# Linear attention on one core: K and V of the last two groups in one load each, Q group by group

## The chip, the core and the metric

The kernel runs on one core of a Trainium2 chip. A core has a matrix engine (TensorE, PE in the profile), three engines for elementwise work (VectorE or DVE, ScalarE or ACT, GpSimd or POOL), and SyncE (SP), which here only issues transfers. Sixteen DMA engines move data between device memory (HBM) and the on-chip memory (SBUF). The engines run side by side and wait for each other through semaphores. The metric is the device time of one execution in microseconds (us); lower is better.

## The reference

Attention without a softmax: Q and K pass through a feature map, and the sums over the sequence are taken first.

```python
# Q, K, V: (8, 12, 512, 64) float32
Q_feat = np.maximum(0, Q) + 1
K_feat = np.maximum(0, K) + 1
KV = np.einsum('bhkd,bhkv->bhdv', K_feat, V)
K_sum = np.sum(K_feat, axis=2)
numerator = np.einsum('bhqd,bhdv->bhqv', Q_feat, KV)
denominator = np.einsum('bhqd,bhd->bhq', Q_feat, K_sum)
return (numerator / (denominator[:, :, :, None] + 1e-10)).astype(np.float32)
```

For each of the 96 heads, K and V give one 64x64 matrix and one vector of 64; Q is multiplied by both, and the first result is divided by the second.

## The kernel before

The 96 heads are worked off in 12 groups of eight heads (`NG` = 12). One group of Q, K or V is 1 MB of float32 in HBM; the load converts it to bf16, so 512 KB arrive in SBUF. One group of the output is 1 MB of float32.

**Loads.** `load` (lines 93 to 103) starts one transfer per tensor from the POOL queue, in the order K, V, Q, for one group or for two at once. The destination is half of a tile, or a whole one, of a pool with two buffers for each tensor (`IN_BUFS` = 2); a tile holds two groups, so a pair of groups reuses the buffer of the pair before the last. `load_pair(s)` (line 105) loads groups 2s and 2s + 1: for the pairs 1 to 4 with one transfer for each tensor (2 MB read), for the last pair, groups 10 and 11, group by group: K10, V10, Q10, K11, V11, Q11, each 1 MB read. (Group 0's K is loaded as float32 from SP by `load_first_k`; V and Q of group 0 and all of group 1 are transfers of their own at the start.) A transfer on the POOL queue has one of eight semaphores, which are used in turn, so a transfer may be issued only when the eighth one before it has landed.

**Work of a group g.** `k_features` and `q_features` (two DVE instructions each, line 122), `v_blocks` (V copied into a block layout, three copies on DVE, line 140, and one on ACT, line 138), `keys_values` (32 matmuls into PSUM, line 157, then ACT moves the sums into `kva_diag`), `transposes` (16 on PE, line 176, each half copied by ACT, line 177), `output` (four times: matmuls into PSUM, line 189, then on DVE a reciprocal, line 199, and a multiplication into `o_sb`, line 200). There are two PSUM buffers for the four parts of `output`, so parts three and four need DVE to be done with parts one and two.

**Order.** The program order is written out by hand under `tc.manual_schedule()`, and each engine follows it strictly. In step g of the main loop the calls are: K features, V blocks and Q features of g, transposes of g - 1, output of g - 2, keys-and-values of g, then (after odd g) the load of the pair that takes the freed buffers, then the store of g - 3. So the loads of groups 10 and 11 stand after the work of step 7. The last group is written out after the loop, with its Q features moved behind the output of group 9.

**Stores.** `store(g)` sends groups 0 to 9 from the POOL queue as one transfer each, and groups 10 and 11 from SP in two halves each. `o_sb` has six buffers (`OUT_BUFS`).

The pair tile is split by `own(g)`; the users of a group wait for the transfer that brought it:

```python
            nc.gpsimd.dma_start(
                out=t[:, ms], in_=drams[x][:, 2 * groups[0] : 2 * groups[-1] + 2]
            )
            for g in groups:
                raw[x, g] = t[:, own(g)]
```

Of the kernel before, what the change touches and what calls it, by code (L numbers as in the profile page):

```python
# [19 lines left out]
def kernel(  # L20
# [64 lines left out]
    def own(g):  # L85
        return slice(g % 2 * 2, g % 2 * 2 + 2)
# [6 lines left out]
    def load(s, groups, names="kvq"):  # L93
        ms = slice(groups[0] % 2 * 2, groups[-1] % 2 * 2 + 2)
        for x in names:
            if (x, "buf", s) not in raw:
                raw[x, "buf", s] = in_pool.tile([P, 4, C2, D], BF16, name=f"{x}_raw")
            t = raw[x, "buf", s]
# [6 lines that stand above are left out]
    def load_pair(s):  # L105
        if s < NG // 2 - 1:
            load(s, (2 * s, 2 * s + 1))
        else:
            load(s, (2 * s,))
            load(s, (2 * s + 1,))  # L110

    def store(g):
        o_sb = outs.pop(g)
# [104 lines left out]
    with tc.manual_schedule():  # L218
# [11 lines left out]
        for t in kva_diag:  # L230
            nc.gpsimd.memset(t, 0.0)
        load_pair(1)
        clear(5, 7, 9)
        for g in range(NG - 1):
            k_features(g)
            v_blocks(g)
            q_features(g)
            if g:
                transposes(g - 1)
            if g >= 2:  # L240
                output(g - 2)
            keys_values(g)
            if g % 2 and g // 2 + 2 < NG // 2:
                load_pair(g // 2 + 2)
            if g >= LAG:
                store(g - LAG)
# [42 lines left out]
```

## Time and profile before

| | before |
|---|---|
| median of 7 runs | 127.21 us (126.61 to 127.89) |
| the profiled execution | 127.06 us |
| its span | 125.3 us |
| granted TensorE clock, mean | 0.823 |
| DVE busy | 88.4 us (71%) |
| ACT busy | 68.0 us (54%) |
| PE busy | 68.2 us (54%) |
| POOL busy | 27.4 us (22%) |
| HBM read, written | 37.75 MB, 12.58 MB (402 GB/s over the span) |

The span is from the first to the last instruction that the profile shows; the execution's own time is 1.8 us longer. A line of the timeline reads: start and duration in us, engine, line of the kernel, operation, destination <- source, shapes, and how many instructions are merged; in brackets, how long the engine had been idle and what ended the wait. For a transfer the duration is that of the issuing instruction, not of the data; when the data landed is asked for separately, by tile. The rows of digits are the share of busy time in 40 equal slices of the span, in tenths; GB/s counts the bytes as written.

### The profile page before, as it was taken

The page shows a single profiled execution, that of the slowest core. Times are in us where ns is not written, and L with a number is a line of the kernel's source. Part 1 is how long each engine was busy: PE and PEld are TensorE (multiplying, and loading weights), DVE is VectorE, ACT ScalarE, POOL GpSimd, SP SyncE. Part 2 cuts the span into 40 slices and gives each one's busy share as a digit, 9 for nine tenths or more (in the row PEclk, how much of TensorE's full clock was granted, in tenths as well). Part 3 has the DMA queues.
Part 4 walks back from the last instruction along what each step waited for, and adds up shares of the span by engine and source line. Part 5 has one row for each costly group of instructions (what it writes and reads, how often), then busy time and mean ns, then how long its engine had stood idle before and what let it go on. Part 6 is the DMA issues. An engine that isn't in the chain of part 4 may idle for free.

```text
span 125.3 us, 2337 instructions
## 1 busy us (share of the span) xinstructions
PE 68.2 (54%) x960; PEld 50.7 (40%) x960; DVE 88.4 (71%) x188; ACT 68.0 (54%) x87; POOL 27.4 (22%) x43
## 2 busy tenths in 40 slices
PE   0005959000049694797847969104978569694500
PEld 0004648000036573556635748003656447482200
DVE  4896280206099998995999985619979999758920
ACT  7832198006700889609796197670079871987000
POOL 6990213000002091020900224203321102020000
PEclk9999999965556999558997799955599967999955
DMA  3999999999999999999999999999999999999993
GB/s 73 343 214 209 211 209 212 213 208 210 210 216 212 211 210 215 212 211 210 242 408 311 209 209 213 211 345 394 228 211 211 213 263 414 421 418 411 402 399 118
DMA packets 13419, 32.13 MB, mean 256 GB/s; under 512 B 608, under 2 KB 608, under 8 KB 13408
## 3 DMA queue, kind: packets, MB, share of 16 engines
q0 software_dynamic: 12048, 28.84, 98.6%
q1 hardware_dynamic: 1360, 3.15, 6.8%
q8 instruction: 7, 0.11, 0.3%
q14 instruction: 4, 0.03, 0.1%
HBM read 37.75 MB, written 12.58 MB: 402 GB/s over the span
## 4 chain that ended last, share of the span: by engine, by line
DMA 69%; DVE 13%; issue 6%; POOL 3%; PE 3%; POOLq 0%; DVEq 0%
DMA out_dram<-o_sb 36%; DMA q_raw<-in_Q_dram 24%; DMA v_raw<-in_V_dram 10%; DVE o_sb L200 8%; DVE v_all L140 2%; POOL v_raw L99 2%; PE kva_ps L157 2%; DVE recip L199 1%; PE qt_ps L176 1%; POOL q_raw L99 1%; PE o_ps L189 1%; POOL out_dram L116 1%; DVE qf L122 1%; DVE kf L122 1%; POOL k_raw L99 0%
## 5 line engine op out<-in xcount | busy, mean ns | idle before, releaser
L157 PE MATMUL kva_ps<-v_all,kf 128*64 128x320 bf16 x384 | 38.4, 370 | 12.2 <-DVE v_all L140 10.7
L189 PE MATMUL o_ps<-kva_diag,qt 128*64 128x130 bf16 x384 | 19.7, 239 | 38.2 <-DVE o_sb L200 37.7
L157 PEld LDWEIGHTS <-kf 128*64 128x64 bf16 x384 | 26.9, 139 | 20.4 <-DVE v_all L140 12.1
L200 DVE TENSOR_TENSOR o_sb<-o_ps,recip 128x512 f32<-128x512 f32 x48 | 33.2, 692 | 1.6
L140 DVE COPY v_all<-v_raw 32x2048 bf16<-32x2048 bf16 x36 | 26.5, 737 | 10.1 <-DMA v_raw<-in_V_dram 9.7
L189 PEld LDWEIGHTS <-qt 128*64 128x64 bf16 x384 | 13.0, 117 | 43.8 <-DVE o_sb L200 42.0
L177 ACT COPY qt<-qt_ps 128x1024 bf16<-128x1024 bf16 x24 | 29.7, 1309 | 0.3
L138 ACT COPY v_all<-v_raw 32x2048 bf16<-32x2048 bf16 x12 | 22.7, 1894 | 11.8 <-DMA v_raw<-in_V_dram 11.6
L167 ACT CAST kva_diag<-kva_ps 64x256 bf16<-64x256 f32 x24 | 8.9, 372 | 34.2 <-PE kva_ps L157 34.1
L122 DVE TENSOR_SCALAR qf<-q_raw 128x1024 bf16<-128x1024 bf16 x24 | 9.1, 423 | 6.5 <-DMA q_raw<-in_Q_dram 6.3
L99 POOL DMA_DIRECT2D k_raw<-in_K_dram x7 | 5.3, 764 | 37.8 <-DVE kf L122 37.8
L176 PE MATMUL qt_ps<-identity,qf 128*128 128x128 bf16 x192 | 13.5, 226 | 0.0
L199 DVE RECIPROCAL recip<-o_ps 128x8 f32<-128x8 f32 x48 | 9.6, 199 | 5.3 <-PE o_ps L189 5.3
L122 DVE TENSOR_SCALAR kf<-k_raw 128x1024 bf16<-128x1024 bf16 x22 | 8.7, 438 | 6.0 <-DMA k_raw<-in_K_dram 6.0
L116 POOL DMA_DIRECT2D out_dram<-o_sb x10 | 8.1, 810 | 21.9 <-DVE o_sb L200 16.3
L176 PEld LDWEIGHTS <-qf 128*128 128x128 bf16 x192 | 11.5, 102 | 3.5 <-issue 3.2
L99 POOL DMA_DIRECT2D v_raw<-in_V_dram x8 | 6.0, 754 | 19.7 <-ACT v_all L138 16.3
L99 POOL DMA_DIRECT2D q_raw<-in_Q_dram x8 | 5.9, 743 | 4.2 <-DMA q_raw<-in_Q_dram 4.2
L213 DVE MEMSET v_all<- 128x3072 f32 (+1 forms) x2 | 4.4, 2192 | 1.1 <-DVE ones L225 0.7
L168 ACT CAST kva_diag<-kva_ps 64x4 bf16<-64x4 f32 x24 | 4.0, 168 | 0.0
L214 ACT COPY v_all<-zero 128x2048 f32<-128x2048 f32 x2 | 3.7, 1894 | 0.0
L214 ACT ACT_TABLE_LOAD x1 | 1.3, 1283 | 0.7 <-PEq L273 0.7
(12 smaller groups left out, 4.6 us busy)
## 6 DMA issues: line engine op xcount, KB each, us to landing
out_dram<-o_sb POOLq DMA_DIRECT2D x10, 1024.0 KB, 19.5
k_raw<-in_K_dram POOLq DMA_DIRECT2D x4, 1024.0 KB, 18.2
v_raw<-in_V_dram POOLq DMA_DIRECT2D x4, 1024.0 KB, 20.6
q_raw<-in_Q_dram POOLq DMA_DIRECT2D x4, 1024.0 KB, 24.7
v_raw<-in_V_dram POOLq DMA_DIRECT2D x4, 512.0 KB, 15.9
q_raw<-in_Q_dram POOLq DMA_DIRECT2D x4, 512.0 KB, 16.7
out_dram<-o_sb SPq DMA_DIRECT2D x4, 512.0 KB, 5.1
k_raw<-in_K_dram POOLq DMA_DIRECT2D x3, 512.0 KB, 22.1
```

Source lines behind the costliest of these rows:

```text
L99: nc.gpsimd.dma_start(out=t[:, ms], in_=drams[x][:, 2 * groups[0] : 2 * groups[-1] + 2])
L116: nc.gpsimd.dma_start(out=o_to, in_=o_sb)
L122: nc.vector.tensor_scalar(out=dst, in0=src, scalar1=1.0, scalar2=1.0, op0=ALU.add, op1=ALU.max)
L138: nc.scalar.copy(out=v_blk[g % 2][ps, b], in_=v_raw[ps])
L140: nc.vector.tensor_copy(out=v_blk[g % 2][ps, b], in_=v_raw[ps])
L157: nc.tensor.matmul(kva_ps[64 * n : 64 * n + 64], lhsT=kf[:, c, n, :], rhs=vb[:, :, n, c, :], start=(c == 0), stop=(c == C2 - 1),)
L167: nc.scalar.copy(out=kva[ps, :, n, 0:D], in_=kva_ps[ps, sb : sb + 4, :])
L176: nc.tensor.transpose(qt_ps[:, c, :], qf[:, half * C + c, :, :], identity)
L177: nc.scalar.copy(out=qt[:, :, :, half], in_=qt_ps)
L189: nc.tensor.matmul(ops[c // 4][64 * j : 64 * j + 64, c // 2 % 2, (c % 2) * W : (c % 2) * W + W], lhsT=qt[:, c, 32 * b : 32 * b + 32, :], r ...
L199: nc.vector.reciprocal(out=recip, in_=cells[:, :, :, :, D:D1])
L200: nc.vector.tensor_tensor(out=o_sb[:, h:NP:2, 4 * i : 4 * i + 4].rearrange("p n (b c) d -> p b c n d", b=2), in0=cells[:, :, :, :, 0:D], i ...
```

## The change

The last pair's six transfers become four: one of 2 MB (as read) for K of groups 10 and 11, one for V of both, then Q of group 10 and Q of group 11 by themselves. The order on the POOL queue is now K10 with K11, V10 with V11, Q10, Q11 instead of K10, V10, Q10, K11, V11, Q11. The bytes, the buffers, the loads of all other groups, and every instruction on DVE, ACT and PE stay as they are and in the same order.

```diff
         if s < NG // 2 - 1:
             load(s, (2 * s, 2 * s + 1))
         else:
-            load(s, (2 * s,))
-            load(s, (2 * s + 1,))
+            load(s, (2 * s, 2 * s + 1), "kv")
+            load(s, (2 * s,), "q")
+            load(s, (2 * s + 1,), "q")
```

## The prediction

> **What bounds the kernel now.** K10 stands for K of group 10, and so on. I read the page's slices and queues first, then the POOL timeline (who issues which transfer when), then DVE and PE near the end.
>
> ```profile
> DMA  3999999999999999999999999999999999999993
> GB/s 73 343 214 209 211 209 212 213 208 210 210 216 212 211 210 215 212 211 210 242 408 311 209 209 213 211 345 394 228 211 211 213 263 414 421 418 411 402 399 118
> q0 software_dynamic: 12048, 28.84, 98.6%
> ```
>
> The DMA engines are full from the second slice to the last but one, and one queue holds nearly all of it. The 210 GB/s of the loads counts bf16 as written; float32 is read, so a group (1 MB read) and a store of 1 MB both cost about 2.5 us. The bytes set a floor, and the change doesn't alter the bytes. What it alters is the order, so I look at the last six loads on POOL:
>
> ```profile
> 69.72 0.71 POOL L99 DMA_DIRECT2D k_raw<-in_K_dram  x1 [6.99 <-DVE kf L122]
> 74.54 0.72 POOL L99 DMA_DIRECT2D v_raw<-in_V_dram  x1 [4.11 <-ACT v_all L138]
> 75.26 0.70 POOL L99 DMA_DIRECT2D q_raw<-in_Q_dram  x1
> 75.94 0.78 POOL L99 DMA_DIRECT2D k_raw<-in_K_dram  x1
> 79.70 0.70 POOL L99 DMA_DIRECT2D v_raw<-in_V_dram  x1 [2.98 <-DMA v_raw<-in_V_dram]
> 84.64 0.71 POOL L99 DMA_DIRECT2D q_raw<-in_Q_dram  x1 [4.25 <-DMA q_raw<-in_Q_dram]
> 87.28 0.76 POOL L116 DMA_DIRECT2D out_dram<-o_sb  x1 [1.93 <-DMA out_dram<-o_sb]
> ```
>
> Asked tile by tile for the time from issue to landing, the trace gives 22.1, 19.8, 21.5, 23.3, 22.1 and 19.6 us for the six loads. Added to the issue times: K10 at 91.8, V10 94.3, Q10 96.8, K11 99.2, V11 101.8, Q11 104.2. The transfer ahead (store of group 3, issued 61.88, 27.6 us) lands at 89.5, the one behind (store of group 4, 19.5 us) at 106.8. So it is first in, first out, with 20 us of backlog: 14.8 us for six loads, 2.46 each, whenever they were issued.
>
> Then DVE, which does all features, three quarters of the V blocks and all divisions, in program order:
>
> ```profile
> 84.38 0.76 DVE L122 TENSOR_SCALAR qf<-q_raw 128x1024 bf16<-128x1024 bf16 x2 [2.80 <-DMA q_raw<-in_Q_dram]
> 96.30 0.75 DVE L122 TENSOR_SCALAR kf<-k_raw 128x1024 bf16<-128x1024 bf16 x2
> 96.97 2.35 DVE L140 COPY v_all<-v_raw 32x2048 bf16<-32x2048 bf16 x3
> 99.33 0.76 DVE L122 TENSOR_SCALAR qf<-q_raw 128x1024 bf16<-128x1024 bf16 x2
> 100.00 0.20 DVE L199 RECIPROCAL recip<-o_ps 128x8 f32<-128x8 f32 x1
> ...
> 107.24 0.21 DVE L199 RECIPROCAL recip<-o_ps 128x8 f32<-128x8 f32 x1 [0.86 <-PE o_ps L189]
> 110.61 0.75 DVE L122 TENSOR_SCALAR qf<-q_raw 128x1024 bf16<-128x1024 bf16 x2
> ...
> 113.05 0.21 DVE L199 RECIPROCAL recip<-o_ps 128x8 f32<-128x8 f32 x1 [1.69 <-PE o_ps L189]
> 119.17 0.69 DVE L200 TENSOR_TENSOR o_sb<-o_ps,recip 128x512 f32<-128x512 f32 x1
> ```
>
> 84.38 is the last time DVE waits for a load. From there on it is busy but for PE answers that depend on DVE itself. Group 10's V copies start 2.7 us after V10 landed, its Q features 2.6 us after Q10; Q11 waits 6.4 us for DVE. The end is a near tie: the last half store is issued at 119.89 when DVE finishes and lands 4.5 us later, at 124.4.
>
> PE in the same stretch:
>
> ```profile
> 87.31 4.23 PE L157 MATMUL kva_ps<-v_all,kf 128*64 128x320 bf16 x32
> 98.28 0.64 PE L189 MATMUL o_ps<-kva_diag,qt 128*64 128x130 bf16 x16
> 100.98 0.42 PE L189 MATMUL o_ps<-kva_diag,qt 128*64 128x130 bf16 x8 [2.06 <-DVE o_sb L200]
> 102.26 3.59 PE L157 MATMUL kva_ps<-v_all,kf 128*64 128x320 bf16 x32
> 109.32 2.34 PE L157 MATMUL kva_ps<-v_all,kf 128*64 128x320 bf16 x32
> ```
>
> The same 32 matmuls take 2.34, 3.59 or 4.23 us: the granted clock in 101.4 to 104.8 us is 0.50, in 104.8 to 108.2 it is 1.00.
>
> **What the Trainium skill says.** "DMA: Bandwidth & Descriptors", section on queues, rings and completion order: an engine starts a ring's descriptors in ring order and alternates between rows by packet. The equal spacing of the landings agrees. Its section on why a DMA increments its semaphore by 16: only the full count says that the data are there; so half a merged load is of no use early. The same page's section on the anatomy of one DMA (POOL's path) fits 2.0 us per DMA plus bytes over 436 GB/s; this trace shows no such fixed cost in the stream: the double loads of groups 8 and 9 landed at 74.4, 79.4 and 84.4, that is 5.0 us for 2 MB against 2.46 for 1 MB. "TensorE: Matmul & The Clock Gate", on the clock gate: after an idle window of about 3.4 us the clock falls to half; the 0.50 above, after a thin stretch, agrees.
>
> **The change part by part.**
> Two POOL issues go, about 0.72 us each. They lie beside a queue 20 us deep and cost nothing. Later issues come sooner: in the trace V11, Q11 and the store of group 4 wait for the landing of the eighth transfer before them, and two fewer transfers shift those partners. Q11 then goes at about 76.0 instead of 84.64, the store of group 4 at 79.7 and of group 5 at 84.6; all stand in the same full queue. Gain 0, and cover stays while the backlog does. K11's and V11's buffers are free at 69.7 and 74.5, since the waits there are already for group 7's K features and V blocks.
>
> The landings move. Same start 89.5: K10 with K11 +4.8 (as for groups 8 and 9) = 94.3; V10 with V11 +5.0 = 99.2; Q10 +2.46 = 101.7; Q11 104.2; stores from 106.8 as before. K10 is 2.5 us later but ahead of its use at 96.30: nothing. V10 arrives 4.9 us later, Q10 4.9 later. K11 and Q11 gain nothing, as DVE only reaches group 11 after group 10.
>
> On DVE: V copies start at 99.26 instead of 96.97 and end at about 101.6 (ACT's quarter at 99.3 instead of 98.31, 1.89 long, done at 101.2, in time). Queued behind them on DVE: Q features, the division of group 8, everything of group 11. Q features wait for Q10, 101.72 instead of 99.33; so the division starts 2.4 us late. Who waits: PE, since output of group 8 gets its PSUM buffers back from DVE, and keys-and-values of group 10 stand behind it, so they start at 104.66 instead of 102.26.
>
> PE then idles 98.9 to 103.4, 4.4 us instead of 2.06. If the clock windows stay where the trace has them, the half clock lasts one window more, to 108.2. Group 4's block, 51.98 to 56.46 us, ran wholly at a granted clock of 0.50 and took 4.48. At half clock from 104.66 to 108.2 (3.55 of 4.48, 79%), then 21% of 2.34: 4.04 instead of 3.59, so +0.45. Bounds: 0 (windows fall otherwise) and 4.48 - 3.59 = 0.9. I take 0.45. PE's answer ends the 0.86 idle of DVE at 107.24, so DVE is from there 2.85 late. The rest is a chain of DVE and PE handing on to each other (keys-and-values of 11 needs the PSUM buffers DVE frees), with no slack to take it up; the 1.69 idle shifts along.
>
> End: last store issued at 119.89 + 2.85 = 122.74. Before, it took 4.5 to land behind three others and the POOL stores; now the DMA is ahead of DVE. An unqueued transfer on SP's queue: the first K load, 1 MB, took 4.95 from 0.74; half the bytes save about 1.25, hence 3.7 at most as a cold one; the skill's fit named above, made for POOL's path, gives 2.0 + 0.52/0.436 = 3.2 as an estimate. I take 3.5: lands 126.24 against 124.38, +1.86. Bounds: shift 2.3 with 3.2 gives +1.0; shift 3.3 with 4.5 gives +3.3. The profiled execution took 127.06 (span 125.3), so 128.9; the median of the runs is 127.21, 0.15 above it, which I leave within the range.
>
> **The rivals.**
> A: the delay is covered by the DMA backlog. For it: the chain puts 69% on DMA, and the store issued at 110.99 still took 8.3 us. Against: backlog shrinks to about 1 us (4.5 - 3.5) at the last store, and DVE is 2.4 late. It needs DVE's lag to be under about 1.6. Time 127.1.
> B, faster: a merged load sheds fixed cost. At 2.0 us each, two fewer transfers bring Q10 to 97.7, no delay is left, the stores have 4 us less ahead, and the last one lands at 119.89 + 3.5 = 123.4, -1.0: 126.1. It decides from a saving of about 1.9 us on. Against: 5.0 for 2 MB and 2.46 for 1 MB.
> C: more loss. Whole block at half clock, stores still 4.5: +3.3, 130.4. For it: PE's longer idle; against: the last stores meet an emptier queue.
>
> **How the numbers follow.** Forecast 0.78 (own range 128.0 to 130.1), A 0.11, B 0.04, C 0.07. 0.5%, some 0.6 us, is about what a measurement can tell from no change. Forecast and C are slower by more, with a little of the forecast's lower edge inside: slower 0.84, same 0.12, faster 0.04. The range leaves out B, most of A and part of C: 127.7 to 130.2.
>
> **What would show it.** V copies of group 10 waiting for the V load to about 99.2, its Q features for Q to about 101.7; Q11 issued near 76; keys-and-values of group 10 starting near 104.7 and taking about 4.0; last division ending near 122.7; the last store landing in about 3.5; GB/s thinning in the last slices. Wrong, if merged loads land in clearly under 4.8 us, or DVE ends before 121.

## The result and the profile after

| | before | after |
|---|---|---|
| median | 127.11 us (33 runs, 126.61 to 127.89) | 128.44 us (14 runs, 127.52 to 129.29) |
| ratio after / before | | 1.0092, 95% interval 1.0070 to 1.0115 |
| profiled execution, its span | 127.06, 125.3 us | 127.52, 125.7 us |
| last store issued, landed | 119.89, 124.4 us | 121.85, 124.8 us |

The changed kernel is slower by 0.9%, 1.2 us by the ratio. Here and below, medians are taken over all executions, while a ratio is worked out without those over 1.5% above the fastest of their kernel and isn't the quotient of the two medians; the two can differ by 0.3%. The profiled execution of the changed kernel is the fastest of its 14, so a second one is read further down.

The line numbers of `output`, `keys_values` and the rest are one higher than before. The page's slices and the row of SP's stores of the kernel after:

```profile
DMA  3999999999999999999999999999999999999984
GB/s 95 329 212 211 210 204 205 209 209 213 211 211 212 212 212 211 214 212 210 245 416 302 210 212 212 210 366 384 212 209 214 211 282 418 421 421 401 360 345 170
...
out_dram<-o_sb SPq DMA_DIRECT2D x4, 512.0 KB, 3.1
```

Before, the last four slices moved 411, 402, 399 and 118 GB/s; now 401, 360, 345 and 170, while the DMA row hardly shows it. SP's stores land 3.1 us after issue (median; 5.1 before): the later ones no longer queue behind other stores, they wait for DVE.

POOL's timeline after. Its brackets name what released an issue:

```profile
68.98 0.75 POOL L99 DMA_DIRECT2D k_raw<-in_K_dram  x1 [6.29 <-DVE kf L123]
73.39 0.75 POOL L99 DMA_DIRECT2D v_raw<-in_V_dram  x1 [3.65 <-ACT v_all L139]
74.13 1.43 POOL L99 DMA_DIRECT2D q_raw<-in_Q_dram  x2
79.42 0.76 POOL L117 DMA_DIRECT2D out_dram<-o_sb  x1 [3.86 <-DMA v_raw<-in_V_dram]
84.64 0.76 POOL L117 DMA_DIRECT2D out_dram<-o_sb  x1 [4.46 <-DMA q_raw<-in_Q_dram]
```

Q11 is issued some 10 us earlier than before and the store of group 4 some 8 us earlier, and neither gains by it: the four loads land at 94.1, 99.0, 101.5 and 104.0 (Q11: 104.2 before), the store at 106.5 (106.8 before).

DVE's timeline after, at the places shown of before:

```profile
95.33 0.75 DVE L123 TENSOR_SCALAR kf<-k_raw 128x1024 bf16<-128x1024 bf16 x2
99.06 2.08 DVE L141 COPY v_all<-v_raw 32x2048 bf16<-32x2048 bf16 x3 [2.98 <-DMA v_raw<-in_V_dram]
101.50 0.76 DVE L123 TENSOR_SCALAR qf<-q_raw 128x1024 bf16<-128x1024 bf16 x2 [0.37 <-DMA q_raw<-in_Q_dram]
102.18 0.20 DVE L200 RECIPROCAL recip<-o_ps 128x8 f32<-128x8 f32 x1
...
109.20 0.21 DVE L200 RECIPROCAL recip<-o_ps 128x8 f32<-128x8 f32 x1 [0.65 <-PE o_ps L190]
115.01 0.21 DVE L200 RECIPROCAL recip<-o_ps 128x8 f32<-128x8 f32 x1 [1.69 <-PE o_ps L190]
...
121.13 0.69 DVE L201 TENSOR_TENSOR o_sb<-o_ps,recip 128x512 f32<-128x512 f32 x1
```

Two waits are new, both on loads of group 10. The division of group 8 starts 2.2 us later than before, and the end of DVE's work is 2.0 us later. PE in the same stretch:

```profile
103.16 0.65 PE L190 MATMUL o_ps<-kva_diag,qt 128*64 128x130 bf16 x8 [5.21 <-DVE o_sb L201]
104.44 3.38 PE L158 MATMUL kva_ps<-v_all,kf 128*64 128x320 bf16 x32
```

Followed back from DVE's last instruction, the chain of this profile passes from DVE to PE and back, step by step, to the landing of Q10:

```profile
74.13 27.35 DMA q_raw<-in_Q_dram
101.50 0.04 DVE qf L123
```

### The profile page after: what moved, and what is told of

It reads as the page before. It is cut to its first block, busy times and chain, and to the rows that moved or that the text cites. A ratio compares the mean times of both kernels' runs of the same rounds, so it can differ in the third digit from the quotient of the medians.

```text
span 125.7 us, 2334 instructions
## 1 busy us (share of the span) xinstructions
PE 68.2 (54%) x960; PEld 50.1 (40%) x960; DVE 88.2 (70%) x188; ACT 68.0 (54%) x87; POOL 26.6 (21%) x41
## 4 chain that ended last, share of the span: by engine, by line
DMA 42%; DVE 27%; PE 17%; POOL 6%; issue 5%; DVEq 0%; POOLq 0%
DMA q_raw<-in_Q_dram 42%; DVE o_sb L201 15%; PE kva_ps L158 11%; DVE v_all L141 4%; PE qt_ps L177 3%; DVE recip L200 3%; PE o_ps L190 3%; POOL v_raw L99 2%; DVE qf L123 2%; DVE kf L123 2%; POOL q_raw L99 1%; POOL kva_diag L232 1%; POOL k_raw L99 1%; POOL identity masks.py:199 0%; POOL identity masks.py:197 0%
## 5 line engine op out<-in xcount | busy, mean ns | idle before, releaser
L190 PE MATMUL o_ps<-kva_diag,qt 128*64 128x130 bf16 x384 | 20.2, 243 | 39.9 <-DVE o_sb L201 39.4
L117 POOL DMA_DIRECT2D out_dram<-o_sb x10 | 8.6, 862 | 33.6 <-DVE o_sb L201 25.3
L177 PE MATMUL qt_ps<-identity,qf 128*128 128x128 bf16 x192 | 13.0, 221 | 0.0
L99 POOL DMA_DIRECT2D k_raw<-in_K_dram x6 | 4.6, 767 | 36.5 <-DVE kf L123 36.5
L177 PEld LDWEIGHTS <-qf 128*128 128x128 bf16 x192 | 10.9, 99 | 3.3 <-issue 3.0
L99 POOL DMA_DIRECT2D v_raw<-in_V_dram x7 | 5.4, 776 | 16.3 <-ACT v_all L139 12.5
```

The source lines that it names most:

```text
L99: nc.gpsimd.dma_start(out=t[:, ms], in_=drams[x][:, 2 * groups[0] : 2 * groups[-1] + 2])
L117: nc.gpsimd.dma_start(out=o_to, in_=o_sb)
L177: nc.tensor.transpose(qt_ps[:, c, :], qf[:, half * C + c, :, :], identity)
L190: nc.tensor.matmul(ops[c // 4][64 * j : 64 * j + 64, c // 2 % 2, (c % 2) * W : (c % 2) * W + W], lhsT=qt[:, c, 32 * b : 32 * b + 32, :], r ...
```

## The experiments

Every ratio is to the kernel before, on the same chip. Where a diff of the last pair's loads has no lines with a minus, the two `load` lines that it replaces aren't shown.

### One merge at a time

K alone merged:

```diff
-            load(s, (2 * s, 2 * s + 1), "kv")
-            load(s, (2 * s,), "q")
-            load(s, (2 * s + 1,), "q")
+            load(s, (2 * s, 2 * s + 1), "k")
+            load(s, (2 * s,), "vq")
+            load(s, (2 * s + 1,), "vq")
```

> Only K of groups 10 and 11 is merged, V and Q go group by group (K10 with K11, V10, Q10, V11, Q11). Theory (the cost is V10 and Q10 arriving late for DVE): V10 lands at 89.3 + 4.8 + 2.5 = 96.6, Q10 at 99.1, against uses at about 97.0 and 99.3 in the kernel before, so no new wait: ratio 1.000 (within 0.3%), about 127.1 us. Rival (a 2 MB transfer in the last pair, or the shifted semaphore partners, cost by themselves): half of the loss or more stays, 127.8 or above.

Measured: 127.37 us, ratio 1.0003 (0.9981 to 1.0026). V alone merged:

```diff
+            load(s, (2 * s,), "k")
+            load(s, (2 * s, 2 * s + 1), "v")
+            load(s, (2 * s,), "q")
+            load(s, (2 * s + 1,), "kq")
```

> Only V of groups 10 and 11 is merged (K10, V10 with V11, Q10, K11, Q11). Theory: V10 lands at 89.3 + 2.4 + 5.0 = 96.7 and Q10 at 99.2, both just ahead of their uses at 97.0 and 99.3: ratio 1.000 (within 0.4%), about 127.1 us, though with the two merges together at +1.2%. Rival (each merge brings its share of the loss): about 127.8 us.

Measured: 127.17 us, ratio 0.9990 (0.9966 to 1.0014). So neither merge costs anything alone that these intervals (about 0.25% either way) can tell. DVE's timeline of the kernel with V alone merged shows how close it is:

```profile
94.84 0.75 DVE L124 TENSOR_SCALAR kf<-k_raw 128x1024 bf16<-128x1024 bf16 x2
96.72 2.07 DVE L142 COPY v_all<-v_raw 32x2048 bf16<-32x2048 bf16 x3 [1.13 <-DMA v_raw<-in_V_dram]
99.19 0.76 DVE L124 TENSOR_SCALAR qf<-q_raw 128x1024 bf16<-128x1024 bf16 x2 [0.39 <-DMA q_raw<-in_Q_dram]
```

DVE waits for V and Q here, but no longer than it was early in this execution: both start within 0.3 us of where the kernel before started them (96.97 and 99.33). Each merge uses up the 2.5 us that the loads were ahead; the second one then costs.

### The order without the merge

```diff
+            for x in "kvq":
+                load(s, (2 * s,), x)
+                load(s, (2 * s + 1,), x)
```

> No transfer is merged; six loads of 1 MB in the order of the changed kernel: K10, K11, V10, V11, Q10, Q11. Theory: V10 lands at about 96.7 and costs nothing, but Q10 lands at 101.6 and DVE waits about 2 us for it; the division of group 8 begins as late as in the changed kernel (about 102.2), so the time is the changed kernel's, 128.4 us (128.0 to 128.8). Rival (merging is what costs): 127.1 us.

Measured: 128.37 us, ratio 1.0072 (1.0051 to 1.0094); the interval overlaps that of the change. With six loads of 1 MB in the changed order:

```profile
96.89 2.08 DVE L141 COPY v_all<-v_raw 32x2048 bf16<-32x2048 bf16 x3 [0.49 <-DMA v_raw<-in_V_dram]
101.92 0.76 DVE L123 TENSOR_SCALAR qf<-q_raw 128x1024 bf16<-128x1024 bf16 x2 [2.95 <-DMA q_raw<-in_Q_dram]
```

V is nearly in time, and Q holds DVE to about the same place as in the changed kernel (101.92 against 101.50). The transfer size isn't the cause; the place of Q10 in the queue is.

### A longer wait

```diff
+            load(s, (2 * s, 2 * s + 1), "k")
+            load(s, (2 * s,), "q")
+            load(s, (2 * s, 2 * s + 1), "v")
+            load(s, (2 * s + 1,), "q")
```

> K and V merged, but Q10 goes ahead of V: K10 with K11, Q10, V10 with V11, Q11. The two MB of V now land at about 101.6 and Q10 early, at 96.6. DVE copies V (2.1 us) only from 101.6 on, then takes Q features: the division of group 8 begins at about 104.4, 2.2 us later than in the changed kernel. Theory (DVE's delay counts in full once the stores are no longer queued): 2.0 to 2.6 us above the changed kernel, 130.4 to 131.0 us. Rival (the stores' backlog still absorbs part of it): 129 to 130 us.

Measured: 130.0 us, ratio 1.0211 (1.0166 to 1.0256), so 1.5 us above the changed kernel, less than the 2.0 expected and at the upper end of the rival's 129 to 130. V is copied from 101.42 on, after a wait of 4.54 us, and the last store is issued at 123.79, 1.9 us later than in the first profile of the changed kernel; its landing, 126.6, is 1.8 later. Between these two profiles a late DVE counts nearly in full, and the last store lands in 2.8 us, so no backlog is left there to absorb any of it. The medians differ by somewhat less; the second profile of the changed kernel, below, shows that its first is an early one.

### Filling the wait

The changed loads; in step 10 the output of group 8 goes ahead of group 10's V blocks:

```diff
             k_features(g)
+            if g == NG - 2:
+                output(g - 2)
             v_blocks(g)
             q_features(g)
             if g:
                 transposes(g - 1)
-            if g >= 2:
+            if g >= 2 and g != NG - 2:
                 output(g - 2)
```

> The changed loads, but in step 10 the output of group 8 (its matmuls and DVE's division) stands ahead of group 10's V blocks, so DVE has 3.4 us of work while V10 and Q10 are on their way. Theory (the loss is DVE standing idle for V10): the waits of 3.0 and 0.4 us in step 10 vanish, DVE ends near 119.8 as in the kernel before, and the time is 127.1 us again (ratio 0.997 to 1.003). Rival (the loss comes from the transfers or from the DMA stream): the time stays at 128.4.

Measured: 127.26 us, ratio 1.0003 (0.9975 to 1.0032). The loss is gone with the loads still merged, but not quite as expected:

```profile
97.63 0.21 DVE L200 RECIPROCAL recip<-o_ps 128x8 f32<-128x8 f32 x1 [0.57 <-PE o_ps L190]
100.99 2.32 DVE L141 COPY v_all<-v_raw 32x2048 bf16<-32x2048 bf16 x3
103.34 0.76 DVE L123 TENSOR_SCALAR qf<-q_raw 128x1024 bf16<-128x1024 bf16 x2
...
108.73 0.21 DVE L200 RECIPROCAL recip<-o_ps 128x8 f32<-128x8 f32 x1 [1.97 <-PE o_ps L190]
```

No wait for a load is left in the step. A later wait for PE grew to 1.97 us, as keys-and-values of group 10 now waits for V copies that come behind the division. In this profiled execution (128.04 us, above the median) Q10 also landed only at 102.8. The last store went out at 121.39, not near 119.8, and took 4.0 us to land. So what this run shows is that the loss can be had back by work put into the wait, not that DVE ends as early as before: in this profile it ends 1.5 us late.

### Is the end DVE's or the transfers'?

The same move in steps 8 and 10, with the loads of the kernel before:

```diff
+            if g in (NG - 4, NG - 2):
+                output(g - 2)
...
-            if g >= 2:
+            if g >= 2 and g not in (NG - 4, NG - 2):
```

> The loads of the kernel before, with the output of groups 6 and 8 ahead of the V blocks of groups 8 and 10. DVE's two waits in step 8 (2.5 us for V, 2.8 us for Q) are partly filled with division, and DVE ends about 3 us earlier. Theory (before the change the stores' stream sets the end and DVE's last store only just follows it): 3 us of DVE bring little, since about 124 us of transfers remain: ratio 0.994 to 0.999, 126.4 to 127.0 us. Rival (DVE's end sets the time also before the change): 124 to 125 us.

Measured: 127.32 us, ratio 1.0001 (0.9977 to 1.0026). DVE ends earlier and no gain is measured; the upper part of the little that was expected (0.994 to 0.999) lies within the interval:

```profile
117.81 0.69 DVE L200 TENSOR_TENSOR o_sb<-o_ps,recip 128x512 f32<-128x512 f32 x1
```

```profile
DMA to landing us min/median/max: 6.0/6.7/7.3
```

The first line is DVE's last, 1.4 us earlier than before; the second, from the view of SP's stores, shows that they only queue longer. Before the change the transfers set the end.

The other direction: the loads of the kernel before, and DVE made late in step 10 by copying one V block again.

```diff
-                nc.vector.tensor_copy(out=v_blk[g % 2][ps, b], in_=v_raw[ps])
+                for _ in range(3 if b == 2 and g == NG - 2 else 1):
+                    nc.vector.tensor_copy(out=v_blk[g % 2][ps, b], in_=v_raw[ps])
```

> The kernel before with its loads untouched; in step 10 DVE copies one V block two times more (same source, same place), which makes it about 1.4 us late (2 x 0.7). Theory (up to about 1.5 us of DVE's lateness is covered, since the last store then takes 3.0 us to land instead of 4.5): ratio 1.000 to 1.004, at most 127.7 us. Rival (no cover, each us of DVE counts): 1.011, 128.6 us.

Measured: 127.59 us, ratio 1.0022 (1.0005 to 1.0039): within what was expected. Its profile shows the cover: the division starts at 101.20, 1.2 us late, PE's block of 32 takes 4.48 us instead of 3.59, so the last store is issued at 122.02, 2.1 us late; it lands in 2.8 us, at 124.8, only 0.4 later than before. With 5 in place of 3:

> The same with four more copies: about 2.8 us late, near the changed kernel's lateness (2.0 and 3.4 us in its two profiles) but with the loads of the kernel before. Theory: 2.8 - 1.5 = 1.3 us, ratio 1.008 to 1.013, as the changed kernel. Rival (the loss comes from the loads' order in the DMA stream, not from DVE being late): 1.000 to 1.004.

Measured: 128.08 us, ratio 1.0045 (1.0021 to 1.0069), under the expected range and under the change. A late DVE alone makes the kernel slower, with the order of the loads untouched; by the ratios that is 0.57 us, about half of the change's 1.17. The rival's range (up to 1.004) lies partly in the interval, so this run alone doesn't exclude that the order of the loads costs something by itself; the filled wait, which has that order and no loss, speaks against it. The profiled execution of this kernel issues its last store at 122.12, about as late as the first profile of the changed kernel. Its step 10 began early (K features at 95.53, 96.30 before), so its division, at 102.12, is 2.1 us late and not 2.8. Why the kernel as a whole stays below the changed one is open.

### PE's clock

The block of 32 matmuls of group 10 took 3.38 us in the first profile after. A second run of the changed kernel:

> The changed kernel itself, on the same chip as the other three, as their base and for a second profile. Its median of 128.4 lies 0.9 above its first profiled execution (127.5). Theory (the rest of the loss is PE's clock in step 10): an execution nearer to 128.4 shows keys-and-values of group 10 longer than 3.38 us, by about its excess. Rival (the rest lies in landings or in the last stores): the block is as long, and landings or the last store are later.

Measured: 128.84 us, ratio 1.0104 (1.0055 to 1.0153). Its profiled execution took 128.98 us; PE and DVE there:

```profile
104.84 4.41 PE L158 MATMUL kva_ps<-v_all,kf 128*64 128x320 bf16 x32
```

```profile
110.64 0.21 DVE L200 RECIPROCAL recip<-o_ps 128x8 f32<-128x8 f32 x1 [1.68 <-PE o_ps L190]
```

The block is 1.03 us longer, the wait of DVE for PE behind it 1.03 us longer (1.68 against 0.65), and the last store, at 123.33, 1.5 us later; most of the remaining 0.4 is Q10, which landed at 101.9 instead of 101.5. So the difference between these two executions comes for the most part from this block.

The granted clock shows why. Between 97 and 112 us it is 0.50 for 3.4 us in the first profile, from 103.1 to 106.5, and for 6.8 us in the second, from 102.3 to 109.1, which covers nearly the whole block. In these traces half clock comes in stretches of 3.4 us. In the kernel before, the 3.4 us ahead of it hold 1.34 us of PE work; in the second profile they hold 0.12, and since the first stretch at half clock holds only 1.94, a second one follows. In the first profile that stretch holds 3.14, and full clock returns.

To take the half clock away, matmuls of the identity into unused PSUM columns were put into PE's wait in step 10 of the changed kernel, 64 of them (36 in a second kernel, so that they end within the wait at half clock too):

```diff
-    def output(g):
+    def output(g, warm=0):
...
+            for _ in range(warm * (1 - h)):
+                nc.tensor.matmul(
+                    ops[1][:, 1, 264:392], lhsT=identity, rhs=identity, start=True, stop=True
+                )
...
-                output(g - 2)
+                output(g - 2, 64 if g == NG - 2 else 0)
```

> The changed kernel with 64 extra matmuls of the identity into unused PSUM columns, put on PE in the 5.2 us in which it waits for DVE in step 10 (they leave the result as it is). They take about 3.6 us at full clock and keep PE from idling. Theory (the half clock after the idle makes keys-and-values of group 10 longer, 3.4 us in the profile, up to 4.5 in others, against 2.34 at full clock, and nothing hides it): 0.7 to 1.3 us below the changed kernel, 127.1 to 127.7. Rival (the clock has no share in the loss): equal to the changed kernel, 128.4.

Measured: 128.73 us, ratio 1.0090 (1.0055 to 1.0125). PE's timeline of its profiled execution (127.91 us):

```profile
98.25 3.75 PE L198 MATMUL o_ps<-identity 128*128 128x128 bf16 x64
103.84 0.42 PE L190 MATMUL o_ps<-kva_diag,qt 128*64 128x130 bf16 x8 [1.84 <-DVE o_sb L205]
104.93 2.34 PE L158 MATMUL kva_ps<-v_all,kf 128*64 128x320 bf16 x32
```

Here the granted clock was 1.00 from 97 to 112 us, the block ran at 2.34 us and DVE's wait behind it was gone, and yet the median isn't lower.

> The changed kernel with 36 extra matmuls of the identity instead of 64. [...]Theory (a warm clock shortens keys-and-values of group 10 and the 64 lost that again in executions that began at half clock): 0.4 to 1.0 us below the changed kernel, ratio to before 1.002 to 1.007. Rival (the clock's share of the loss is small): 1.009 to 1.011 as with 64 or none.

Measured: 128.56 us, ratio 1.0089 (1.0063 to 1.0116): the rival's value. In its profiled execution, at 129.64 us far above the median, the 36 matmuls took 2.18 us and the block still 4.01: they ended at 101.0, from 101.5 on 3.4 us held 0.93 us of PE work, and then half clock came. So they didn't do in every execution what they were put there for. That a faster block would bring the median down is not shown; only single executions show the block's length passed on to the end.

## Why the prediction held, point by point

**Landings.** Forecast 94.3, 99.2, 101.7 and 104.2; measured 94.1, 99.0, 101.5, 104.0. First in, first out held, and so did the pace. Two issues less and the earlier issues brought nothing, as the sum had it. That a merged load sheds a fixed cost (rival B) is out: the K load took 4.8 us of the stream and V 4.9.

**DVE.** V copies at 99.06 and Q features at 101.50 (forecast 99.26 and 101.72), the division 2.2 us late (forecast 2.4). That this wait is the cause rests on two runs: the order alone brings a ratio of 1.0072 without the merge, and work put into the wait takes it away with the merge in place. A DVE made late by extra copies brings about half as much, so the size isn't accounted for in full.

**PE's clock, +0.45.** The second stretch of half clock that the forecast added is in most traces (the kernels with extra matmuls aside). Where DVE was late in step 10, the half clock between 97 and 112 us lasts 6.8 us in five of six profiles; only the first of the changed kernel has 3.4. Where DVE wasn't late it lasts 3.4 us in all five (before, K alone, V alone, both moved divisions). What didn't hold is that the stretches stay where the trace before has them: in the six late profiles they start anywhere from 100.4 to 103.1, and the block starts later too, so that part of it can lie behind them. The block took 3.30 to 4.48 us when DVE was late (4.48 with two more copies) and 3.40 to 4.01 when it wasn't; a longer block in the changed kernel than in the kernel before isn't shown. Nor did the half clock before follow an idle window of 3.4 us: PE's longest gap ahead of it was 2.06 us. The sum's 2.85 us of lateness lies between the 2.0 and 3.4 of the two profiles of the changed kernel.

**The last store, the term that was mis-sized.** Set at 3.5 us, bounded below by 3.2, it measured 3.0 in both profiles, and 2.8 in the kernel with the longer wait. The estimates came from a cold load (4.9 us in the trace) and from a fit made for POOL's path. The backlog thus covers 1.5 us of DVE's lateness instead of 1.0. By the mean of the two profiles, 2.7 us of lateness less 1.5 gives 1.2 us, which is what the ratio gives; with two executions, so close a fit is partly luck. The forecast's +1.86 is too high mostly by this term. With the store at 3.0 the forecast would have been +1.4 with the clock's 0.45 and +0.9 without it, so the total doesn't tell whether the 0.45 belongs there. In the first profile, 1.96 less 1.52 leaves 0.44, the 0.46 us between the two profiled executions.

**The rivals.** A, all covered, would have been right under about 1.5 us of lateness: K alone, V alone and the filled wait are such cases, at ratios of 0.9990 to 1.0003. C's longer store didn't happen in the two profiles; its whole block at nearly half clock did, in the second.

**Not settled.** The rest between the kernel with four more copies and the changed one, some 0.6 us by the ratios, whose intervals (1.0021 to 1.0069 and 1.0070 to 1.0115) only just miss each other, and how large the clock's share is in the median.

No version tried beats the kernel before: with DVE ahead, the transfers end at the same time.

## What to carry to other kernels

Behind a full queue that served first in, first out, an earlier issue was worth nothing here and the order decided: put each load at the landing time that its first user needs, and count what every transfer ahead of it adds. A merge delays the part that is needed first by the part that isn't; one such delay can disappear in slack and a second on top of it cost in full, so single edits that measure as free don't add up. At the end, compare the time at which the last producer finishes with the transfer backlog at that moment: until the backlog is used up lateness is free (about 1.5 us here), and beyond it nearly every microsecond counted between the profiles of the changed kernel and of the longer wait.

## What was not expected of the hardware

The last store, 512 KB from SP with no queue ahead, landed in 2.8 to 3.0 us in the profiles of the changed kernel, of the order alone and of the longer wait; in the profile with 36 extra matmuls it took 4.2. The same block of 32 matmuls of group 10 took anything from 2.34 us (granted clock 1.00 throughout) to 4.48 (0.50 throughout), and between two executions of one kernel 3.38 and 4.41. In all twelve profiles that show half clock between 97 and 112 us, it lasted 3.4 or 6.8 us; it came after 3.4 us that held at most 1.34 us of PE work. One load of 1 MB, Q10 in the kernel with the filled wait, took 3.3 us of the stream where others take 2.5, and everything behind it landed later by that 0.8.
